# The RMSNorm gain as a per-partition scale where transposed activations leave PSUM, and the first loads in a new order on two queues

## The chip, the cores and the metric

One core of one Trainium2 chip runs the whole kernel. The metric is the device time of one execution in microseconds (us).

## What is computed

A decoder trunk of two layers on x with 256 rows (tokens) and 1024 columns, float32. What this change touches is the norm at the head of each layer and the products that read it:

```
for l in range(DEPTH):                       # 2
    h = rms_norm(x, norm_g[l])               # x * rsqrt(mean(x*x) + eps) * g
    proj = h @ w_in[l]                       # split into q, kv, gates, ... for four token mixers
    outs = (nsa(...), conv(...), stick_breaking(...), s5(...))   # each times silu of a gate
    mixed = sum over m of sigmoid(merge[m]) * (outs[m] @ w_branch[l, m])
    x = x + mixed @ w_out[l]
```

## The kernel before

The engines have short names in the profile: PE is TensorE, ACT is ScalarE, DVE is VectorE, POOL is GpSimd, and SP issues most loads. The 256 tokens are two tiles of 128 partitions, called t=0 and t=1. Weights come in 78 tiles a layer of 512 KB (`raw`, three buffers). Each is split into two parts: a rounded copy `hi` (ACT, L148) and the remainder `lo` = raw - hi (L150), on DVE or, for tiles 2, 4, 79, 81 and 95, on POOL. A product of activations and weights is three matmuls, hi by hi, lo by hi and hi by lo. A load for a buffer waits until the remainder three tiles earlier is done.

The head of a layer goes through these steps for each of its two token tiles:

- `norm_square` adds up the squares of a row (ACT, L533), with halves of 512 columns in layer 0 and quarters of 256 in layer 1, as the output projection of the layer before delivers them. DVE adds the parts (L538), POOL raises the sum to the power -1/2 (L539).
- `norm_scale` (L547) makes h = x * rs * g on DVE, in two halves of 512 columns. The gain g lies in `ng`, a 128x1024 tile that a load has broadcast over all partitions.
- `norm_transpose` turns the eight 128x128 pieces of h on PE (L555) into two PSUM banks `hT`, four pieces in each. Per bank, ACT rounds 128x512 into `hh` (L558), and DVE puts the remainder of the same bank into `hl` (L559). `hh` and `hl` are what every projection reads.

The projection reads q first, then ksw (keys), then vsw (values) and so on. Query and key outputs are then normed, rotated and transposed: ACT squares (L565), DVE sums (L567), POOL takes the power (`rsq`, `rsk`, L569), DVE multiplies (L576 to L587), PE transposes into `qTp` and `kTp` (L592), and the first scores are `sc` (L703).

The order of SP and POOL is the program's own. The order of PE, DVE and ACT is set by a scheduler of the framework, which runs a model of the timeline when the kernel is built. Each engine executes its list in order. At the start the loads are issued by SP one after another: x in two halves, constants, positions, gain and weights in turns. PE meanwhile runs 13 matmuls on zeros.

Of the kernel before, what the change touches and what calls it, by code (L numbers as in the profile page):

```python
# [31 lines left out]
# columns of the input projection  # L32
# [3 lines left out]
# parameters packed per partition  # L36
# [9 lines left out]
_CS = [("ident", 128), ("invf", 32), ("tau", 32)]  # L46
# [15 lines left out]
def slot_plan():  # L62
    """The weight tiles in the order of their use: (key, kind, columns)."""
# [51 lines left out]
class Weights:  # L115
    """Streams the weight tiles and splits each into two float32r parts."""
# [40 lines left out]
    def advance(self, g):  # L157
        """Emits the splits of the tiles after tile g, as far as the tiles in use leave room."""
        end = min(g + self.depth - 1, min(self.parts_in_use, default=g) + self.depth, DEPTH * NSLOT)
        while self.ns < end:  # L160
            self.prefetch(self.ns + 1)
            self._split()
        self.prefetch(min(max(self.ns, g + 1) + self.ahead, DEPTH * NSLOT))
# [14 lines left out]
def tile_hybrid_trunk(ctx: ExitStack, tc: tile.TileContext, x, pos, cst, msk, wq, ws, ng, pk, w1, gw, out):  # L178
# [25 lines left out]
    def stack(name, parts):  # L204
        """For each of the four groups of 32 rows, those rows of the three parts one below the other."""
        out = []
        for pair in range(2):
            t = fp.tile([96, 2, 512], F32R, name=f"{name}{pair}", tag="f")
            for j in range(2):
                q = 2 * pair + j  # L210
                for i, part in enumerate(parts):
                    nc.sync.dma_start(t[32 * i:32 * i + 32, j, :].bitcast(F32),
                                      part[32 * q:32 * q + 32].bitcast(F32))
            out.append(t)
        return out
# [54 lines left out]
    # tiles with blocks that stay zero  # L270
# [7 lines left out]
    # rotary tables: [token, (tile 0, tile 1, compressed), 2, 32]  # L278
# [43 lines left out]
    def load_ng(l, L):  # L322
        L["ng"] = fp.tile([P, D], F32, name=f"ng{l}", tag="f")
        nc.sync.dma_start(L["ng"], ng[l:l + 1, :].to_broadcast([P, D]))
# [31 lines left out]
    def prep_s5(l, L):  # L356
        """Phases of the state rotation; the decay and the output matrices."""
# [39 lines left out]
    def prep_s5_tables(l, L):  # L397
        """Rotation by 16 i + j steps, from those by 16 i and by j."""
# [126 lines left out]
    def norm_square(l, t, u, n):  # L525
        """Adds up the squares of the u-th of n parts of a row."""
# [5 lines left out]
        with tc.high_priority():  # L532
            A.activation(h[:, cols], xs[:, t, cols], AF.Square, scale=1.0 / 32, accum_out=ss[:, u:u + 1])  # L533
# [8 lines left out]
    def norm_scale(l, t):  # L542
        h, rs = Ls[l]["norm"][t]
        for c in range(2):
            cols = slice(c * 512, c * 512 + 512)
            with tc.high_priority():
                V.scalar_tensor_tensor(h[:, cols], xs[:, t, cols], rs, Ls[l]["ng"][:, cols], op0=ALU.mult, op1=ALU.mult)  # L547

    def norm_transpose(l, t, act):
        hh, hl = act  # L550
        h = Ls[l]["norm"][t][0]
        for c in range(2):
# [3 lines left out]
            dst = (slice(None), slice(4 * c, 4 * c + 4), slice(t * P, (t + 1) * P))  # L556
            with tc.high_priority():
                A.copy(hh[dst], ps)  # L558
                V.tensor_sub(hl[dst], ps, hh[dst].bitcast(F32))  # L559

# [1 line left out]
    def nsa_rope(l, t, name, ps, L, kinds, scale, dst):  # L562
        """QK norm, rotation and transposition of four heads; kinds: the gain rows of the heads."""
# [127 lines left out]
    def nsa_full(l, L, acc, t, bs):  # L691
        """Causal attention of the branches bs (0 selected, 1 window) for query tile t."""
# [290 lines left out]
    def prepare(l):  # L983
        """What a layer needs apart from its activations."""
# [9 lines left out]
    ng0 = fp.tile([P, D], F32, name="ng0", tag="f")  # L994
    Ls[0]["ng"] = ng0
    halves = [slice(c * 512, c * 512 + 512) for c in range(2)]
    for c in halves:
        nc.sync.dma_start(xs[:, 0, c], x[0:P, c])
    nc.sync.dma_start(cs, cst)
    nc.sync.dma_start(posi, pos)  # L1000
    nc.sync.dma_start(ng0[:, halves[0]], ng[0:1, halves[0]].to_broadcast([P, 512]))
    W.prefetch(1)
    nc.sync.dma_start(ng0[:, halves[1]], ng[0:1, halves[1]].to_broadcast([P, 512]))
# [33 lines left out]
    for l in range(DEPTH):  # L1037
# [82 lines left out]
        if more:  # L1120
            load_ng(l + 1, Ls[l + 1])
# [24 lines left out]
def _constants():  # L1146
# [3 lines left out]
    def put(n, v):  # L1150
        o, w = CS[n]
        c[:v.shape[0], o:o + w] = v

    put("ident", np.eye(P))
    inv = np.power(10000.0, -np.arange(32) / 32).astype(np.float32)
# [12 lines left out]
def _layout(x, positions, norm_g, w_in, nsa_qk_g, nsa_cmp_pe, nsa_cmp_w1, nsa_cmp_w2, sc_conv_w, s5_a_re, s5_a_im,  # L1168
            s5_log_dt, s5_b_re, s5_b_im, s5_c_re, s5_c_im, s5_d, s5_glu_w, s5_glu_b, w_branch, w_out):
    Ld = DEPTH  # L1170
    cst, msk = _constants()
# [52 lines left out]
    arrays = dict(x=x[0], pos=pos, cst=cst, msk=msk, wq=wq, ws=ws, ng=norm_g, pk=pk, w1=w1, gw=gw)  # L1224
# [22 lines left out]
```

## Time and profile before

| What | us |
| --- | --- |
| Runs | 583.56, 584.46, 586.82 |
| Median of the runs | 584.46 |
| Profiled execution, first to last instruction | 583.8 |
| PE busy | 553.6 (95%) |
| DVE busy | 435.6 (75%) |
| POOL busy | 283.0 (48%) |
| ACT busy | 266.4 (46%) |

The profiled execution's own device time is not listed apart from its span. The mean granted clock of PE over the span is 0.976. Timelines give the start of an instruction, counted from the first one, its duration, what it is, and in brackets how long its engine had been idle before it and what ended that. Matmuls are pipelined, so the step from one start to the next is the pace, not the duration. [...]

### The profile page before, as it was taken

The numbers are of one execution on the slowest core, as the hardware profiler recorded it, in microseconds if no ns is written. First come the engines' busy times: TensorE is split into PE (matmuls) and PEld (weight loads), VectorE is DVE, ScalarE is ACT, GpSimd is POOL, SyncE is SP. The second block draws the span as 40 slices with busy tenths as digits, with TensorE's granted clock in tenths as the row PEclk, the third lists the DMA queues.
The fourth block names the chain that finished last, engine by engine and source line by source line (L and its number), as shares of the span: only waits on it lengthen the run. The fifth ranks groups of instructions, "written<-read, shape, count | busy, mean of one in ns | idle before, by whom it ended". The sixth has DMA issues, their size and how long they took to land.

```text
span 583.8 us, 11199 instructions
## 1 busy us (share of the span) xinstructions
PE 553.6 (95%) x4417; PEld 515.9 (88%) x4417; DVE 435.6 (75%) x649; ACT 266.4 (46%) x438; POOL 283.0 (48%) x314
## 2 busy tenths in 40 slices
PE   6897999999799999969798999999999999999997
PEld 3897988889598899969698999889889899999997
DVE  3997776898898676786469974859999685677782
ACT  4658453544243446424254474633534354444440
POOL 3699835546554476899934420214356500132230
PEclk8997999999899999979899999999999999999999
DMA  8664153534345364545444653454334456555531
GB/s 266 224 227 142 38 199 116 192 113 170 115 144 183 108 232 146 187 159 175 153 149 133 233 177 96 145 164 154 131 125 138 170 169 197 186 183 177 207 129 56
DMA packets 28709, 93.54 MB, mean 160 GB/s; under 512 B 3824, under 2 KB 5104, under 8 KB 28656
## 3 DMA queue, kind: packets, MB, share of 16 engines
q1 hardware_dynamic: 28656, 92.82, 47.1%
q8 instruction: 35, 0.57, 0.4%
q14 instruction: 18, 0.15, 0.1%
HBM read 88.61 MB, written 1.05 MB: 154 GB/s over the span
## 4 chain that ended last, share of the span: by engine, by line
PE 65%; POOL 19%; DVE 7%; issue 6%; DMA 2%; ACT 1%; SPq 0%; DVEq 0%; POOLq 0%; ACTq 0%
PE mg L492 19%; PE wo L482 6%; PE br L937 5%; PE z L492 4%; POOL cy L289 3%; PE sbk L492 2%; PE s5u L492 2%; PE sbv L482 2%; PE xin L492 2%; PE cg L492 2%; PE bg L492 2%; PE sc L703 2%; POOL mt L286 2%; PE nsacc L740 2%; POOL cy L286 2%
## 5 line engine op out<-in xcount | busy, mean ns | idle before, releaser
L150 DVE TENSOR_TENSOR lo<-raw,hi 128x1024 fp32r<-128x1024 f32 (+1 forms) x151 | 202.3, 1345 | 44.3 <-ACT hi L148 44.1
L148 ACT CAST hi<-raw 128x1024 fp32r<-128x1024 f32 (+1 forms) x154 | 161.0, 1049 | 153.8 <-PE mg L492 56.9
L492 PE MATMUL mg<-hh,hi 128*128 128x256 f32 x512 | 146.0, 285 | 5.6 <-DVE mt L940 5.6
L492 PE MATMUL mg<-hh,lo 128*128 128x256 f32 x512 | 145.2, 284 | 0.0
L492 PE MATMUL mg<-hl,hi 128*128 128x256 f32 x512 | 145.1, 283 | 0.0
L492 PEld LDWEIGHTS mg<-hh,hi 128*128 128x128 f32 x512 | 97.9, 191 | 11.0 <-DVE mt L940 5.8
L492 PEld LDWEIGHTS mg<-hh,lo 128*128 128x128 f32 x512 | 97.5, 190 | 0.4 <-issue 0.4
L492 PEld LDWEIGHTS mg<-hl,hi 128*128 128x128 f32 x512 | 97.4, 190 | 0.4 <-issue 0.4
L286 POOL TENSOR_TENSOR mt<-mt,mt 128x512 f32<-128x512 f32 x14 | 22.9, 1633 | 78.8 <-DVE mt L940 78.8
L482 PE MATMUL wo<-hi,mx 128*128 128x256 f32 x256 | 48.1, 288 | 4.1 <-ACT mx L956 4.1
L289 POOL TENSOR_TENSOR cy<-cy 128x256 f32<-128x256 f32 x16 | 23.0, 1437 | 52.9 <-DVE cy L865 49.1
L482 PEld LDWEIGHTS wo<-hi,mx 128*128 128x128 f32 x256 | 40.8, 194 | 4.7 <-ACT mx L956 4.5
L937 PE MATMUL br<-oh,hi 128*128 128x256 f32 x128 | 36.0, 281 | 0.5 <-ACT g L922 0.5
L492 PE MATMUL z<-hl,hi 128*128 128x256 f32 x128 | 36.2, 283 | 0.0
L492 PE MATMUL z<-hh,lo 128*128 128x256 f32 x128 | 36.1, 282 | 0.0
L492 PE MATMUL z<-hh,hi 128*128 128x256 f32 x128 | 36.0, 281 | 0.0
L937 PE MATMUL br<-oh,lo 128*128 128x256 f32 x128 | 36.0, 281 | 0.0
L937 PE MATMUL br<-ol,hi 128*128 128x256 f32 x128 | 35.9, 281 | 0.0
L482 PE MATMUL wo<-lo,mx 128*128 128x256 f32 x128 | 35.9, 286 | 0.0
L286 POOL TENSOR_TENSOR s5a<-s5a,s5b 128x256 f32<-128x256 f32 x16 | 19.6, 1222 | 26.3 <-DMA raw<-in_ws_dram 13.9
L859 DVE TENSOR_TENSOR_SCAN s5b<-r,s5a 128x256 f32<-128x256 f32 x32 | 20.3, 677 | 14.2 <-POOL s5a L289 14.2
L492 PEld LDWEIGHTS z<-hl,hi 128*128 128x128 f32 x128 | 24.1, 188 | 0.8 <-issue 0.8
(334 smaller groups left out, 1430.2 us busy)
## 6 DMA issues: line engine op xcount, KB each, us to landing
raw<-in_ws_dram SPq DMA_DIRECT2D x152, 512.0 KB, 3.9
raw<-in_wq_dram SPq DMA_DIRECT2D x4, 536.0 KB, 4.9
w<-in_w_dram SPq DMA_DIRECT2D x4, 512.0 KB, 6.1
b<-bh SPq DMA_DIRECT2D x16, 64.0 KB, 2.0
u<-uh SPq DMA_DIRECT2D x16, 64.0 KB, 2.0
gw<-in_gw_dram SPq DMA_DIRECT2D x2, 512.0 KB, 5.5
out_dram<-xs SPq DMA_DIRECT2D x8, 128.0 KB, 1.7
pk<-in_pk_dram SPq DMA_DIRECT2D x2, 322.0 KB, 3.5
```

The lines of the kernel that those rows point to most:

```text
L148: self.nc.scalar.copy(hi[:, :w], t[:, :w])
L150: sub.tensor_sub(lo[:, :w], t[:, :w], hi[:, :w].bitcast(F32))
L286: G.tensor_add(o, a, b)
L289: G.tensor_sub(o, a, b)
L482: T.matmul(ps[:, :width], lhsT=act(4 * h + kk)[ia][:, tt], rhs=w[iw][:, kk, :], start=n == 0, stop=n == last)
L492: T.matmul(ps, lhsT=w[:, k, :], rhs=a[:, k, :], start=n == 0, stop=n == last)
L703: T.matmul(sc[kh].rearrange("p (b g k) -> p b g k", b=nb, g=2)[:, :, g, :], lhsT=qT[iq][rows[kh], g, t * P:(t + 1) * P], rhs=kT[ik][rows[k ...
L740: T.matmul(acc[rows[kh], :, t * P:(t + 1) * P], lhsT=v[:, c, b * P + 64 * kh:b * P + 64 * kh + 64], rhs=ps4[kh][:, c, 2 * i:2 * i + 2, :], ...
L859: V.tensor_tensor_scan(y[:, ri, :], L["r"][:, pr:pr + 1].to_broadcast([P, S]), a[:, ri, :], 0.0, op0=ALU.mult, op1=ALU.add)
L937: T.matmul(ps[:, j, :], lhsT=w[:, 2 * m + k, :], rhs=a[:, k, :], start=n == 0, stop=n == 5)
```

## The change

- The gain is 16 more columns in the table of constants `cs` (192 to 208 columns): column 8l+k holds for each partition the gain of piece k of layer l. The tile `ng` and its loads go, 512 KB a layer.
- h becomes x * rs alone, a TENSOR_SCALAR.
- `norm_transpose` applies the gain where a piece leaves PSUM: per piece one ACT copy of 128x128 with the gain as scale and one DVE instruction hT * g - hh. There are 32 and 32 of them where there were 8 and 8.
- In layer 0 the square of the second half goes from ACT to DVE.
- Loads at the start: the second half of x on ACT's queue, and the first two weight tiles earlier on SP's.

```diff
-_CS = [("ident", 128), ("invf", 32), ("tau", 32)]
+_CS = [("ident", 128), ("gain", 16), ("invf", 32), ("tau", 32)]
...
-    def load_ng(l, L):
-        L["ng"] = fp.tile([P, D], F32, name=f"ng{l}", tag="f")
-        nc.sync.dma_start(L["ng"], ng[l:l + 1, :].to_broadcast([P, D]))
...
         with tc.high_priority():
-            A.activation(h[:, cols], xs[:, t, cols], AF.Square, scale=1.0 / 32, accum_out=ss[:, u:u + 1])
+            if l == 0 and u == 1:
+                V.scalar_tensor_tensor(h[:, cols], xs[:, t, cols], 1.0 / D, xs[:, t, cols], op0=ALU.mult, op1=ALU.mult,
+                                       accum_out=ss[:, u:u + 1])
+            else:
+                A.activation(h[:, cols], xs[:, t, cols], AF.Square, scale=1.0 / 32, accum_out=ss[:, u:u + 1])
...
             with tc.high_priority():
-                V.scalar_tensor_tensor(h[:, cols], xs[:, t, cols], rs, Ls[l]["ng"][:, cols], op0=ALU.mult, op1=ALU.mult)
+                V.tensor_scalar(h[:, cols], xs[:, t, cols], rs, None, op0=ALU.mult)
...
-            dst = (slice(None), slice(4 * c, 4 * c + 4), slice(t * P, (t + 1) * P))
             with tc.high_priority():
-                A.copy(hh[dst], ps)
-                V.tensor_sub(hl[dst], ps, hh[dst].bitcast(F32))
+                for k in range(4):
+                    g = C("gain")[:, 8 * l + 4 * c + k:8 * l + 4 * c + k + 1]
+                    hi, lo = (v[:, 4 * c + k, t * P:(t + 1) * P] for v in (hh, hl))
+                    A.activation(hi, ps[:, k, :], AF.Copy, scale=g)
+                    V.scalar_tensor_tensor(lo, ps[:, k, :], g, hi.bitcast(F32), op0=ALU.mult, op1=ALU.subtract)
...
-    ng0 = fp.tile([P, D], F32, name="ng0", tag="f")
-    Ls[0]["ng"] = ng0
-    halves = [slice(c * 512, c * 512 + 512) for c in range(2)]
-    for c in halves:
-        nc.sync.dma_start(xs[:, 0, c], x[0:P, c])
+    nc.sync.dma_start(xs[:, 0, :512], x[0:P, :512])
+    nc.scalar.dma_start(xs[:, 0, 512:], x[0:P, 512:])
     nc.sync.dma_start(cs, cst)
+    W.prefetch(1)
     nc.sync.dma_start(posi, pos)
-    nc.sync.dma_start(ng0[:, halves[0]], ng[0:1, halves[0]].to_broadcast([P, 512]))
-    W.prefetch(1)
-    nc.sync.dma_start(ng0[:, halves[1]], ng[0:1, halves[1]].to_broadcast([P, 512]))
     W.prefetch(2)
...
-        if more:
-            load_ng(l + 1, Ls[l + 1])
+    put("gain", norm_g.reshape(DEPTH, KC, P).transpose(2, 0, 1).reshape(P, -1))
```

The scheduler orders PE, DVE and ACT anew around the head of each layer; POOL's list keeps its order. In the new list of PE, 139 matmuls stand ahead of the first transposition of a key tile (kTp00) and 269 ahead of the second (kTp01), the 13 on zeros counted; before, they were 192 and 249. Ahead of the first scores stand 277 (before 279). Two places follow.

DVE in layer 0, from the remainders of t=0 on (the first two digits behind a name are layer and token tile, hT000 and hT001 are the two banks of t=0; lo0, lo1, lo3 are remainders of weight tiles). Before:

```order
L559 TENSOR_TENSOR hl0_153<-hT000_162,hh0_152 128x4x128 [waits Activation_49]
L559 TENSOR_TENSOR hl0_153<-hT001_169,hh0_152 128x4x128 [waits Activation_49]
L312 TENSOR_SCALAR ang_184<-ang_184 128x96 [waits Pool_49]
L150 TENSOR_TENSOR lo1_198<-raw1_127,hi1_197 128x1072 [waits DMAHW7_49,Activation_49]
L538 SCALAR_TENSOR_TENSOR ss01_204<-ss01_204 128x1 [waits Activation_49]
L319 TENSOR_SCALAR ropeS_112<-ropeS_112 128x3x32 [waits Activation_49]
L547 SCALAR_TENSOR_TENSOR h01_203<-xs_93,ss01_204,ng0_118 128x512 [waits DMAHW0_49,Pool_49]
L547 SCALAR_TENSOR_TENSOR h01_203<-xs_93,ss01_204,ng0_118 128x512
```

and now, from the third piece (of pieces 0 to 3 of a bank) of t=0 on:

```order
L538 SCALAR_TENSOR_TENSOR ss01_213<-ss01_213 128x1 [waits DVE_49,Activation_49]
L561 SCALAR_TENSOR_TENSOR hl0_150<-hT000_159,cs_94,hh0_149 128x128 [waits Activation_49]
L547 TENSOR_SCALAR h01_212<-xs_93,ss01_213 128x512 [waits Pool_49]
L547 TENSOR_SCALAR h01_212<-xs_93,ss01_213 128x512
L561 SCALAR_TENSOR_TENSOR hl0_150<-hT001_172,cs_94,hh0_149 128x128 [waits Activation_49]
L319 TENSOR_SCALAR ropeS_112<-ropeS_112 128x3x32 [waits Activation_49]
L561 SCALAR_TENSOR_TENSOR hl0_150<-hT000_159,cs_94,hh0_149 128x128 [waits Activation_49]
L341 TENSOR_TENSOR gS0_236<-qk0_129,ropeS_112 128x192 [waits DMAHW0_49,DVE_49]
L341 TENSOR_TENSOR gS0_236<-qk0_129,ropeS_112 128x192
L342 TENSOR_TENSOR gS0_236<-qk0_129,ropeS_112 128x64
L150 TENSOR_TENSOR lo3_254<-raw3_189,hi3_253 128x1024 [waits DMAHW1_49,Activation_49]
L561 SCALAR_TENSOR_TENSOR hl0_150<-hT001_172,cs_94,hh0_149 128x128 [waits Activation_49]
```

Both remainders of t=0 stood ahead of h of t=1 (h01); now three of the eight stand behind it.

DVE at the boundary of the layers (hT100 and hT101 are the two banks of t=0 in layer 1, h11 is h of t=1, lo82 a weight remainder). Before:

```order
L965 SCALAR_TENSOR_TENSOR xs_93<-wo031_3708,xs_93 128x256 [waits PE_49]
L559 TENSOR_TENSOR hl1_3667<-hT100_3721,hh1_3666 128x4x128 [waits Activation_49]
L559 TENSOR_TENSOR hl1_3667<-hT101_3728,hh1_3666 128x4x128 [waits Activation_49]
L538 SCALAR_TENSOR_TENSOR ss11_3527<-ss11_3527 128x1 [waits Activation_49]
L547 SCALAR_TENSOR_TENSOR h11_3526<-xs_93,ss11_3527,ng1_3454 128x512 [waits Pool_49]
L547 SCALAR_TENSOR_TENSOR h11_3526<-xs_93,ss11_3527,ng1_3454 128x512 [waits DVE_49]
L150 TENSOR_TENSOR lo82_3770<-raw82_3704,hi82_3769 128x1024 [waits DMAHW2_49,Activation_49]
```

and now, from the small sum for t=1 on, which follows the second piece of both banks:

```order
L538 SCALAR_TENSOR_TENSOR ss11_3546<-ss11_3546 128x1 [waits Activation_49]
L561 SCALAR_TENSOR_TENSOR hl1_3686<-hT100_3740,cs_94,hh1_3685 128x128 [waits Activation_49]
L561 SCALAR_TENSOR_TENSOR hl1_3686<-hT101_3753,cs_94,hh1_3685 128x128 [waits Activation_49]
L547 TENSOR_SCALAR h11_3545<-xs_93,ss11_3546 128x512 [waits Pool_49]
L547 TENSOR_SCALAR h11_3545<-xs_93,ss11_3546 128x512 [waits DVE_49]
L150 TENSOR_TENSOR lo82_3801<-raw82_3723,hi82_3800 128x1024 [waits DMAHW7_49,Activation_49]
L561 SCALAR_TENSOR_TENSOR hl1_3686<-hT100_3740,cs_94,hh1_3685 128x128 [waits Activation_49]
L561 SCALAR_TENSOR_TENSOR hl1_3686<-hT101_3753,cs_94,hh1_3685 128x128 [waits Activation_49]
```

The last piece of each bank of t=0 now follows h11 and lo82.

## Rows read from the trace of the kernel before

**Rows 1.** The page: the span.

```profile
span 583.8 us, 11199 instructions
```

**Rows 2.** Stretches: us, busy time and count of each engine, clock, share of DMA, GB/s.

```profile
51.00:54.00 3.00, 3.00 (x15) 2.50 (x15) 2.93 (x8) 1.87 (x3) 2.92 (x4) 0.50 0.51 171
...
156.70:160.10 3.40, 3.40 (x11) 1.55 (x12) 3.37 (x5) 0.62 (x1) 2.03 (x3) 0.50 0.44 154
303.00:308.00 5.00, 5.00 (x44) 5.00 (x44) 2.65 (x4) 2.65 (x4) 2.08 (x2) 1.00 0.33 111
```

**Rows 3.** Timeline of PE, start to 51 us: start, duration, instruction, count, idle before it.

```profile
11.95 1.24 PE L482 MATMUL q<-hi,hh 128*128 128x268 f32 x4
...
44.88 0.41 PE L592 MATMUL kTp<-cs,m1k 128*128 128x128 f32 x2 [1.14 <-DVE m1k L587]
...
45.25 0.28 PE L492 MATMUL sbq<-hh,lo 128*128 128x256 f32 x1
...
48.19 0.28 PE L492 MATMUL sbk<-hh,hi 128*128 128x256 f32 x1
...
50.82 0.58 PE L703 MATMUL sc<-kT,qT 64*128 64x256 f32 x1 [2.23 <-DVE qTl L595]
```

**Rows 4.** Timeline of ACT, first 10 us.

```profile
4.47 0.63 ACT L533 ACTIVATE h<-xs 128x512 f32<-128x512 f32 x1 [0.36 <-DMA xs<-in_x_dram]
...
9.24 1.08 ACT L148 CAST hi<-raw 128x1072 fp32r<-128x1072 f32 x1 [4.05 <-DMA raw<-in_wq_dram]
```

**Rows 5.** Timeline of DVE, first 25 us.

```profile
8.08 0.75 DVE L547 SCALAR_TENSOR_TENSOR h<-xs,ss,ng 128x512 f32<-128x512 f32 x1 [2.70 <-DMA ng<-in_ng_dram]
...
12.23 1.41 DVE L559 TENSOR_TENSOR hl<-hT,hh 128x512 fp32r<-128x512 f32 x2
...
16.01 3.52 DVE L547 SCALAR_TENSOR_TENSOR h<-xs,ss,ng 128x512 f32<-128x512 f32 x2 [0.44 <-POOL ss L539]
...
22.79 1.66 DVE L318 COPY ropeC<-ropeC 128x96 f32<-128x96 f32 x1
```

**Rows 6.** Groups of lines of ACT, then DVE: busy us, mean ns of one, idle before.

```profile
L715 ACT ACTIVATE e<-sc,m 128x128 f32<-128x128 f32 x16 | 5.7, 373 | 1.3 <-DVE m L711 1.3
...
L558 ACT CAST hh<-hT 128x512 fp32r<-128x512 f32 x8 | 4.6, 584 | 3.6 <-PE hT L555 3.5
...
L559 DVE TENSOR_TENSOR hl<-hT,hh 128x512 fp32r<-128x512 f32 x8 | 5.3, 682 | 0.5 <-ACT hh L558 0.5
...
L582 DVE TENSOR_TENSOR sqq<-q,gS 128x128 f32<-128x128 f32 x8 | 1.9, 279 | 0.0
...
L906 DVE TENSOR_SCALAR s5th<-s5th 128x512 f32<-128x512 f32 x2 | 0.9, 428 | 2.8 <-ACT s5th L904 2.8
```

**Rows 7.** Timeline of POOL, 16 to 32 us.

```profile
16.32 2.66 POOL L150 TENSOR_TENSOR lo<-raw,hi 128x1024 fp32r<-128x1024 f32 x1 [0.35 <-ACT hi L148]
21.95 2.42 POOL L150 TENSOR_TENSOR lo<-raw,hi 128x1024 fp32r<-128x1024 f32 x1 [2.97 <-ACT hi L148]
...
31.46 2.04 POOL L569 TENSOR_TENSOR rsk<-ssk,mhalf 128x4 f32<-128x4 f32 x1
```

**Rows 8.** Timeline of DVE at the layer boundary.

```profile
305.94 3.68 DVE L547 SCALAR_TENSOR_TENSOR h<-xs,ss,ng 128x512 f32<-128x512 f32 x2 [0.68 <-POOL ss L539]
...
313.98 3.55 DVE L547 SCALAR_TENSOR_TENSOR h<-xs,ss,ng 128x512 f32<-128x512 f32 x2 [0.67 <-POOL ss L539]
317.45 1.22 DVE L150 TENSOR_TENSOR lo<-raw,hi 128x1024 fp32r<-128x1024 f32 x1
```

**Rows 9.** Timeline of POOL at the layer boundary.

```profile
306.49 2.59 POOL L150 TENSOR_TENSOR lo<-raw,hi 128x1072 fp32r<-128x1072 f32 x1 [0.58 <-ACT hi L148]
313.39 0.56 POOL L539 TENSOR_TENSOR ss<-ss,mhalf 128x1 f32<-128x1 f32 x1 [4.31 <-DVE ss L538]
313.91 2.41 POOL L150 TENSOR_TENSOR lo<-raw,hi 128x1024 fp32r<-128x1024 f32 x1
```

**Rows 10.** Timeline of PE at the layer boundary.

```profile
311.97 0.76 PE L482 MATMUL q<-hi,hh 128*128 128x268 f32 x4 [1.57 <-ACT hh L558]
```

More of the change, by code (lines that the diff above doesn't have):

```diff
@@ L177, in tile_hybrid_trunk @@
 @with_exitstack
-def tile_hybrid_trunk(ctx: ExitStack, tc: tile.TileContext, x, pos, cst, msk, wq, ws, ng, pk, w1, gw, out):
+def tile_hybrid_trunk(ctx: ExitStack, tc: tile.TileContext, x, pos, cst, msk, wq, ws, pk, w1, gw, out):
     nc = tc.nc
@@ L1143, in tile_hybrid_trunk, with _constants @@
             W.advance((l + 1) * NSLOT - 1)
-def _constants():
+def _constants(norm_g):
     t = np.arange(P)
@@ L1170, in _layout @@
     Ld = DEPTH
-    cst, msk = _constants()
+    cst, msk = _constants(norm_g)
     p = positions[0]
@@ L1223, in _layout @@
     gw = s5_glu_w.reshape(Ld, 2, P, 512).transpose(0, 2, 1, 3)
-    arrays = dict(x=x[0], pos=pos, cst=cst, msk=msk, wq=wq, ws=ws, ng=norm_g, pk=pk, w1=w1, gw=gw)
+    arrays = dict(x=x[0], pos=pos, cst=cst, msk=msk, wq=wq, ws=ws, pk=pk, w1=w1, gw=gw)
     return {k: np.ascontiguousarray(v) for k, v in arrays.items()}
```

## The prediction

> **What bounds the kernel now.** I read the page first: TensorE (PE) is busy for nearly the whole span of 583.8 us [rows 1], so a change counts only where PE stands still or runs at its lower clock. [...] The timeline of PE shows what came before: the first q matmul at 11.95, then, after a dense run, idle 1.14 us ahead of 44.88 and 2.23 us ahead of 50.82 [rows 3]. At 50.82 the clock falls. It did not fall after the 1.57 us of idle at 311.97, where layer 1 starts [rows 10]. So about 12 us at the start, the gaps at 44 to 51 with what the clock takes behind them, and 1.57 us at the boundary are what the edited lines could move. Everything else is PE at its pace.
>
> The timelines of the feeding engines tell why. At the start h waits for the broadcast gain (idle 2.70 before 8.08), and ScalarE (ACT) waits 4.05 us for the first weight tile [rows 4, 5]. Second, h of t=1 takes 3.52 us for two instructions at 16.01, and 3.68 and 3.55 at the boundary [rows 5, 8], though the first one at 8.08 took 0.75. Beside each long pair lies a POOL remainder of a weight tile (16.32, 306.49, 313.91) [rows 7, 9]: VectorE (DVE) stands until POOL is done. The small COPY at 22.79 does the same: 1.66 us, ending with POOL's 21.95+2.42 [rows 5, 7].
>
> **The change part by part.** The profiled execution's span is 583.8; its own device time is not listed, and the median of the runs, 584.46, lies 0.7 above it. I work in differences and add them to 584.46. All results inside 0.5% (2.92 us) are "same": a measurement of this kernel can hardly tell them from none.
>
> *Gain loads gone, first loads reordered.* Both halves of x are there at about 4.0 (the second was used at 4.47 [rows 4]). Squares run side by side on ACT and DVE to about 4.9; with the power on POOL (0.56 [rows 9]) h can start at 5.8. As TENSOR_SCALAR a half takes 0.43 (the L906 row [rows 6]), so h is done at 6.6 where it was 11.1. The transposes follow the warm-up, the first weight tile, which came 1.16 us behind the gain's first half (9.24 against 8.08 [rows 4, 5]), now follows the constants, by my estimate at 6 to 6.5, and q starts near 8.3 instead of 11.95: 3.6 us ahead. The gain load that goes at the boundary I cost at nothing: h waits there 0.68 for POOL, not for it [rows 8].
>
> *The copies out of PSUM.* Before, a bank took one ACT copy and one DVE subtraction of 512 columns. Now each takes four and four of 128, and in the order every further ACT copy of a bank waits for DVE's last one on it. No row has these forms. The ACT copy: below, a quarter of the whole-bank copy (0.584, L558), 0.15; above, 0.37, that of 128 columns with a per-partition operand (L715). I take 0.37, the nearest form. DVE: 0.28 (128x128, L582) to 0.68 (the whole bank, L559); I take 0.34, near the first [rows 6]. A step of one bank is then 0.37+0.34 and two hand-overs, about 0.8 (DVE waits 0.67 for a power that takes 0.56, so two cost 0.1 [rows 8, 9]); four steps of two interleaved banks are 3.2 to 3.6 us a tile. Before, hi-copy and subtraction of a tile overlapped in about 1.9. Alone that is 1.5 us for each of four tiles, and a gain of zero is the other end if other work fills the steps. What decides is what DVE has *between* these steps, since it runs in order.
>
> *Start, the sum.* DVE's order from q's start: remainder of tile 0 to 8.4 (its cast is done by 7.1, the remainder takes 1.2 to 1.3), piece 0 of both banks to 9.1, remainder 1 behind its cast to 10.7, the square of t=1 (0.75 taken for it, as for h) to 11.5, piece 1 to 12.2, the small sum, piece 2 of the first bank to 12.9. The power that follows the sum costs 0.67 [rows 8], so h of t=1 can start at 13.2 (16.01 before). POOL has its tile 2 ready at that time and takes it first, for 2.4 us. DVE stands, h of t=1 ends at 16.5 (19.53 before). Behind it in the order stand the last remainders of t=0: with the rope products and weight tile 3 ahead of the final one, that is ready at about 20.4, where all of t=0's were at 13.64 [rows 5]. Then gC and eight remainders of t=1 with the q and k work between: the last at about 33. POOL's power for k, behind its chain of phases, starts at 32.3 (31.46 before) and takes 2.04 [rows 7], so k's rotated tile, a product of some 0.4 later, is there at about 34.8. In the order that transposition of k (kTp00) has 139 matmuls ahead of it. Before, the 249 that stand ahead of kTp01 were done at 43.74, the start of the idle time at 44.88; at 0.118 each (25 steps from 45.25 to 48.19 [rows 3]) PE had done 173 at 34.8. The new kernel is 34 matmuls, 4.0 us, behind.
>
> But it then has no gap to fall into: from 34.8 the 138 matmuls to the first score take 16.3, to 51.1, about when its inputs come (50.82 before). In the kernel before the clock is low from there for nearly 7 us, and PE does 5 matmuls a us instead of 8.8, a loss of 3.0 [rows 2]. Kept high, PE ends 2.7 ahead. Against that I set one stretch of 3.4 us at the low clock (as at 156.7 [rows 2]), worth 1.7, for the stalls before 35. **Start: -1.0**, bounds -4 (h of t=1 not held up) and +3 (two long low stretches, 2x3.0 against the 2.7).
>
> *Boundary.* h of t=0 now needs 2x0.43 from 305.94, done before POOL's tile 79 can hold it: 2.8 us gained on DVE. It lets the square of t=1, the cast of tile 81 and so the first copy move to 309.6, and q starts at 310.4, as soon as PE has ended wo: the 1.57 us go. Then the steps bite. Pieces 0 to 2 of both banks end at 312.9 with DVE's xs, its remainders and the square in between. The order then has h of t=1 (two), weight remainder 82, and only behind these the remainders of piece 3. At about 312.6 POOL's power for t=1 ends and POOL goes straight into its tile 81, whose cast I put at 309.5, as it did before at 313.91, 0.07 us ahead of h's start at 313.98 [rows 8, 9]. h is held to 315.1 and done at 315.9, tile 82 takes 1.22 [rows 8] to 317.1, piece 3's first remainder is there at 317.5. PE meanwhile can issue 22 matmuls from 310.4 and idles twice for about 2.3 us. Before, from 311.97 to 317.45 it issued some 44. That is 22x0.118 = 2.6 us lost, the 1.57 included. With 2.6 us of work in 7 the clock should fall, as it did behind 2.23 us of idle at 50.82; one stretch of 3.4 us costs 1.7. **Boundary: +4.3**, bounds +0.5 (h not held) and +6 (a long low stretch, 3.0, and more stalls in t=1's copies).
>
> [...]
>
> [...]
>
> *Rest of layer 1.* Reordered, no new wait seen: 0, bounds +-1.
>
> **Sum:** 584.46 - 1.0 + 4.3 + 0 = 587.8.
>
> **Rivals.**
> (A) h gets ahead of POOL at the boundary, or the clock stays up there. For it: 0.07 us decided at 313.91. Against it: DVE now arrives later than the power's end, not earlier. Boundary +0.6 or +2.6; with start -1.0 or -2.7 the time is 584.1 or 584.4. The same.
> (B) Faster: the three early microseconds are kept. For it: q starts 3.6 us earlier, and 6.4 us of idle and low clock lie ahead at 44 to 58. It needs tile 2's cast to end after the power of t=1, so that h is done at 14.1 and t=0's last remainder near 18. Start -4, boundary +0.6: 581.0. Its point of decision is whether POOL's tile 2 starts behind h.
> (C) Slower still: the copies starve PE at both places long enough for long low-clock stretches. Start +2, boundary +6: 592.5.
> (D) The change does not do what it says: not open, since the order shows 32 and 32 short copies, no gain load, and TENSOR_SCALAR.
>
> **How the numbers follow.** Forecast 0.40 (0.07 of it within 0.5%), A 0.29, B 0.20, C 0.11. Faster 0.20, same 0.29+0.07 = 0.36, slower 0.33+0.11 = 0.44. The range 580.5 to 592.5 reaches from B to C; the forecast's own is 585.5 to 591.
>
> **What would show it.** Right: q begins near 8.3, the last t=0 remainder comes at 19 to 21, little PE idle at 44 to 51, clock 1.00 from 51 to 57, and around 315 PE waiting for hl over 2 us behind an h of more than 2 us. Wrong: h of t=1 under 0.5 us in either layer, a clock of 1.00 behind the boundary, or copies much off 0.37 and 0.34.

## The result, and the profile after

The changed kernel took 590.58 us, the median of 8 runs (586.05 to 592.28); the kernel before, in 8 runs beside them, 584.59 (583.56 to 586.82). The ratio, taken over all runs, is 1.0084, with a 95% interval of 1.0057 to 1.0110: slower by 0.84% (the two medians alone lie 6.0 us, 1.0%, apart). The median is inside the forecast's own range of 585.5 to 591. The profiled execution took 591.84 with a span of 590.1, 6.3 more than the span of before [rows 1].

The page: the span, and busy time of each engine (share of the span, count).

```profile
span 590.1 us, 11232 instructions
PE 559.4 (95%) x4417; PEld 519.3 (88%) x4417; DVE 435.6 (74%) x677; ACT 270.9 (46%) x458; POOL 284.9 (48%) x314
```

The new forms, in the groups of lines of ACT and DVE (busy us, mean ns of one, idle before and what ended it):

```profile
L560 ACT ACTIVATE hh<-hT,cs 128x128 fp32r<-128x128 f32 x32 | 10.9, 366 | 17.4 <-DVE hl L561 9.6 <-PE hT L555 7.4
...
L561 DVE SCALAR_TENSOR_TENSOR hl<-hT,cs,hh 128x128 fp32r<-128x128 f32 x32 | 10.5, 343 | 4.6 <-ACT hh L560 4.4
L547 DVE TENSOR_SCALAR h<-xs,ss 128x512 f32<-128x512 f32 x8 | 7.7, 1007 | 1.8 <-POOL ss L539 1.8
```

The pieces cost 0.37 and 0.34, as taken [rows 6]. ACT's copies stood idle 17.4 us, 9.6 of it behind DVE: the hand-overs. And h has a mean of 1007 ns where 428 was the free price [rows 6], since two of the four pairs (the two halves of h) were held by POOL (2.99 and 2.97 us; the other two took 0.88).

**The start.** DVE's timeline:

```profile
6.13 0.88 DVE L547 TENSOR_SCALAR h<-xs,ss 128x512 f32<-128x512 f32 x2 [0.75 <-POOL ss L539]
...
14.31 2.99 DVE L547 TENSOR_SCALAR h<-xs,ss 128x512 f32<-128x512 f32 x2 [0.42 <-POOL ss L539]
...
19.67 0.34 DVE L561 SCALAR_TENSOR_TENSOR hl<-hT,cs,hh 128x128 fp32r<-128x128 f32 x1
...
35.15 2.90 DVE L150 TENSOR_TENSOR lo<-raw,hi 128x1024 fp32r<-128x1024 f32 x2
...
39.37 0.15 DVE L570 TENSOR_SCALAR ssq<-ssq 128x4 f32<-128x4 f32 x1
```

POOL's, from 14 us:

```profile
14.23 2.39 POOL L150 TENSOR_TENSOR lo<-raw,hi 128x1024 fp32r<-128x1024 f32 x1
...
39.60 1.01 POOL L571 TENSOR_TENSOR rsq<-ssq,mhalf 128x4 f32<-128x4 f32 x1 [2.64 <-DVE ssq L570]
...
61.37 1.51 POOL L286 TENSOR_TENSOR BB<-bm,bm 64x128 f32<-64x128 f32 x2
```

PE's, from 8 to 63 us:

```profile
8.40 0.39 PE L478 MATMUL q<-hi,hh 128*128 128x268 f32 x1 [0.63 <-ACT hh L560]
10.10 0.39 PE L478 MATMUL q<-hi,hh 128*128 128x268 f32 x1 [1.31 <-ACT hh L560]
...
18.00 0.59 PE L478 MATMUL q<-hi,hl 128*128 128x268 f32 x1 [1.50 <-DVE hl L561]
...
33.60 0.44 PE L594 MATMUL kTp<-cs,m1k 128*128 128x128 f32 x2 [0.78 <-DVE m1k L589]
...
50.26 0.38 PE L705 MATMUL sc<-kT,qT 64*128 64x256 f32 x1
...
62.93 0.53 PE L462 MATMUL bbp<-cs,BB 128*128 128x128 f32 x2 [1.74 <-POOL BB L286]
```

q starts 3.55 us earlier than before [rows 3] and stands after each piece; h of t=1 is held from 14.31 to POOL's end (14.23+2.39) and its second half runs free (0.48); the last remainder of t=0 ends at 20.0; kTp00 comes at 33.60; the first score at 50.26 waits for nothing (2.23 before [rows 3]). That far it is the predicted path. Then the last row: PE stands 1.74 us at 62.93 for BB, a matrix that POOL builds for the s5 mixer. The table of stretches (length, busy time and count of PE, weight loads, DVE, ACT, POOL, granted clock as a share of the full one, share of DMA, GB/s) shows what follows it:

```profile
10.00:20.00 10.00, 5.72 (x20) 4.60 (x21) 8.64 (x19) 6.00 (x14) 6.91 (x8) 0.60 0.61 195
20.00:35.00 15.00, 14.22 (x111) 14.02 (x111) 13.11 (x41) 7.16 (x17) 11.17 (x16) 0.93 0.59 198
35.00:50.00 15.00, 15.00 (x127) 14.87 (x127) 14.04 (x28) 11.55 (x19) 11.94 (x12) 1.00 0.69 220
50.00:58.00 8.00, 7.28 (x54) 6.40 (x53) 7.60 (x19) 6.99 (x17) 7.56 (x13) 1.00 0.34 116
58.00:63.00 5.00, 3.26 (x71) 2.81 (x70) 4.75 (x10) 1.52 (x9) 4.65 (x7) 1.00 0.01 3
63.00:66.50 3.50, 3.50 (x18) 3.50 (x19) 1.71 (x4) 2.13 (x4) 3.34 (x6) 0.52 0.16 37
```

The clock is 1.00 from 50 to 58, where it was 0.50 before [rows 2], but 0.52 from 63 to 66.5, where it was 1.00. That last stretch in the kernel before:

```profile
63.00:66.50 3.50, 3.50 (x32) 3.50 (x31) 2.37 (x6) 1.68 (x3) 3.34 (x6) 1.00 0.00 0
```

**The boundary.** DVE's timeline:

```profile
307.83 0.88 DVE L547 TENSOR_SCALAR h<-xs,ss 128x512 f32<-128x512 f32 x2 [0.68 <-POOL ss L539]
...
309.71 2.48 DVE L150 TENSOR_TENSOR lo<-raw,hi 128x1024 fp32r<-128x1024 f32 x1 [0.66 <-ACT hi L148]
...
314.50 2.97 DVE L547 TENSOR_SCALAR h<-xs,ss 128x512 f32<-128x512 f32 x2
317.40 1.21 DVE L150 TENSOR_TENSOR lo<-raw,hi 128x1024 fp32r<-128x1024 f32 x1
318.53 0.60 DVE L561 SCALAR_TENSOR_TENSOR hl<-hT,cs,hh 128x128 fp32r<-128x128 f32 x2
```

POOL's and, below it, ACT's:

```profile
313.91 0.56 POOL L539 TENSOR_TENSOR ss<-ss,mhalf 128x1 f32<-128x1 f32 x1 [2.81 <-DVE ss L538]
314.44 2.36 POOL L150 TENSOR_TENSOR lo<-raw,hi 128x1024 fp32r<-128x1024 f32 x1
```

```profile
314.70 1.04 ACT L148 CAST hi<-raw 128x1024 fp32r<-128x1024 f32 x1 [0.54 <-DMA raw<-in_ws_dram]
315.65 0.62 ACT L560 ACTIVATE hh<-hT,cs 128x128 fp32r<-128x128 f32 x2
```

PE's, and its stretch at the low clock:

```profile
312.09 0.29 PE L478 MATMUL q<-hi,hh 128*128 128x268 f32 x1
...
316.07 0.59 PE L478 MATMUL q<-hi,hh 128*128 128x268 f32 x1 [1.35 <-ACT hh L560]
...
318.93 0.59 PE L478 MATMUL q<-hi,hl 128*128 128x268 f32 x1 [0.28 <-DVE hl L561]
```

```profile
315.70:322.50 6.80, 6.16 (x27) 5.86 (x27) 3.43 (x5) 0.57 (x3) 1.09 (x1) 0.50 0.43 136
```

h of t=0 is free, q starts without its 1.57 us [rows 10], POOL's tile 81 starts 0.06 us ahead of h of t=1 and holds it to 316.8 (314.44+2.36), so that h ends at 317.5, and the fourth pieces come behind h and tile 82 [compare rows 8, 9]. The hold that h of t=0 had before has moved: the remainder of tile 80 on DVE now starts at 309.71, while POOL is at its tile 79 (308.39 to 311.09), and takes 2.48 us, where that of tile 82 takes 1.21.

To place the loss I count the matmuls that PE has started up to some times, from the same view with stretches that begin at 0; a minus means behind the kernel before. At full clock one is 0.118 us [rows 3]; between 55 and 70 us many are shorter (62 of the changed kernel's, from 58.58 on, take 2.24 us together), so there the first matmul on BB (bbp) serves as the mark, though its place in PE's list moves by up to 12 matmuls between these kernels. g12 is counted without the 4 matmul instructions that spread its gain.

| Kernel (profiled execution) | at 35 | first bbp | at 100 | at 310 | at 550 | started from 310 to 330 |
| --- | --- | --- | --- | --- | --- | --- |
| before, number started | 179 | 62.98 us | 674 | 2221 | 4159 | 146 |
| changed | -28 | 60.75 | -16 | -16 | -52 | 119 |
| e1_whole | +1 | 58.70 | 0 | +4 | +23 | 161 |
| e2_no81 | -32 | 61.16 | -6 | -2 | -40 | 130 |
| e4_l1old | -28 | 61.29 | +5 | +2 | +13 | 153 |
| e6_l0old | +1 | 59.42 | +9 | +6 | -14 | 132 |
| e7_no24 | -8 | 59.04 | +14 | -14 | -48 | 114 |
| e8_81first | -30 | 60.98 | -16 | -12 | -30 | 134 |
| g12_gain_in_psum | +16 | 56.41 | +31 | +23 | +48 | 169 |

The changed kernel is 2.2 us ahead at bbp. The wait of 1.74 us takes most of that, and in the low stretch behind it PE starts 18 matmuls where before it started 32 from 63 to 66.5: 1.7 us. It is 16 behind (1.9 us) at 100 and at 310, loses 27 (3.2 us) in the 20 us of the boundary and 9 more (1.1 us) after it: 6.1 of the 6.3.

### The profile page after: what moved, and what is told of

Read it like the earlier page. It is cut to its first block, busy times and chain, and to the rows that moved or that the text cites. A ratio compares the mean times of both kernels' runs of the same rounds, so it can differ in the third digit from the quotient of the medians.

```text
span 590.1 us, 11232 instructions
## 1 busy us (share of the span) xinstructions
PE 559.4 (95%) x4417; PEld 519.3 (88%) x4417; DVE 435.6 (74%) x677; ACT 270.9 (46%) x458; POOL 284.9 (48%) x314
## 4 chain that ended last, share of the span: by engine, by line
PE 64%; POOL 19%; DVE 9%; issue 4%; DMA 2%; ACT 1%; DVEq 0%; POOLq 0%; ACTq 0%
PE mg L488 20%; PE wo L478 6%; PE z L488 5%; PE br L939 4%; DVE lo L150 3%; POOL mt L286 3%; PE s5u L488 2%; PE sbv L478 2%; PE xin L488 2%; PE bg L488 2%; PE cg L488 2%; POOL cy L289 2%; POOL rot L292 2%; PE nsacc L742 2%; PE sc L705 2%
## 5 line engine op out<-in xcount | busy, mean ns | idle before, releaser
L488 PEld LDWEIGHTS z<-hh,hi 128*128 128x128 f32 x128 | 24.2, 189 | 1.2 <-issue 1.2
```

Source lines behind the costliest of these rows:

```text
L488: T.matmul(ps, lhsT=w[:, k, :], rhs=a[:, k, :], start=n == 0, stop=n == last)
```

## The experiments

Each ratio is against runs of the kernel before on the same chip. Where an experiment keeps the old lines for some token tiles, it also loads the gain for those.

**e1_whole: the change with whole-bank copies.**

```diff
-                for k in range(4):
-                    g = C("gain")[:, 8 * l + 4 * c + k:8 * l + 4 * c + k + 1]
-                    hi, lo = (v[:, 4 * c + k, t * P:(t + 1) * P] for v in (hh, hl))
-                    A.activation(hi, ps[:, k, :], AF.Copy, scale=g)
-                    V.scalar_tensor_tensor(lo, ps[:, k, :], g, hi.bitcast(F32), op0=ALU.mult, op1=ALU.subtract)
+                A.copy(hh[dst], ps)
+                V.tensor_sub(hl[dst], ps, hh[dst].bitcast(F32))
```

(`dst` is the same slice as in the kernel before.)

> The changed kernel with the whole-bank copies of before (one ACT copy and one DVE subtraction of 512 columns a bank); the gain is left out, so its output lacks it. Loads, the short h and the square on DVE stay. Theory H (the short copies of t=0 end up behind h of t=1, which POOL holds, and the clock falls behind the wait): both places recover, h of t=1 is still held about 2.4 us but nothing of t=0 stands behind it; 579 to 583, so 2 to 6 us under the kernel before. Rival L (the loads, the second queue or the extra DVE square cost the time): stays near 590. A gain of zero against the kernel before (584 to 585) would say that the early start is absorbed later.

Measured: 583.52, ratio 0.9982 (0.9959 to 1.0005), a little above the 579 to 583 of its theory. All else that the change does gains at most 0.4%; the pieces, with the order that the scheduler makes around them, cost 0.84 + 0.18 = 1.0%, 6 us. The two were not run apart: kTp00 stands behind 186 matmuls here and behind 139 in the changed kernel. DVE's timeline at the boundary shows where the pieces cost it:

```profile
309.85 0.68 DVE L559 TENSOR_TENSOR hl<-hT,hh 128x512 fp32r<-128x512 f32 x1
...
310.77 0.68 DVE L559 TENSOR_TENSOR hl<-hT,hh 128x512 fp32r<-128x512 f32 x1
...
312.26 3.03 DVE L547 TENSOR_SCALAR h<-xs,ss 128x512 f32<-128x512 f32 x2 [0.67 <-POOL ss L539]
```

h of t=1 is held as long as in the changed kernel, yet PE starts 161 matmuls from 310 to 330 instead of 119: both remainders are out before h. The tile 80 remainder takes 2.48 us here too. So these holds by themselves are not the loss (PE waits 0.64 us for h here, at 315.04, and 0.31 before); they harm most what the pieces leave behind them.

**e4_l1old and e6_l0old: the change in one layer alone.** e4 keeps the old gain and copies in layer 1, e6 all of the old head of layer 0, its loads and both squares on ACT included.

```diff
+OLD = [(1, 0), (1, 1)]
...
+                if (l, t) in OLD:
+                    V.scalar_tensor_tensor(h[:, cols], xs[:, t, cols], rs, Ls[l]["ng"][:, cols], op0=ALU.mult, op1=ALU.mult)
...
+            if (l, t) in OLD:
+                dst = (slice(None), slice(4 * c, 4 * c + 4), slice(t * P, (t + 1) * P))
+                with tc.high_priority():
+                    A.copy(hh[dst], ps)
+                    V.tensor_sub(hl[dst], ps, hh[dst].bitcast(F32))
+                continue
```

For e6 the first line is `OLD = [(0, 0), (0, 1)]`, and the loads of the start stand as before.

> The changed kernel in layer 0; in layer 1 the gain is loaded, multiplied into h and copied by whole banks as before. It takes the boundary's part out. Theory H: the boundary is worth 4.4 us of the 6, so 585.5 to 587, with 1 to 2 us lost at the start, and the clock at 1.00 behind the boundary. Rival C (the short copies cost alike in both layers, 3 us each): 587.5.

> Layer 0 as before (its loads, gain loaded at the start, whole-bank copies, both squares on ACT), layer 1 as changed. It leaves the boundary alone. Theory H: all of the boundary's 3.3 to 4.7 us and none of the start's: 587.5 to 589.5. If start and boundary only add up, this and the run with layer 1 as before together exceed the kernel before by as much as the changed kernel does (about 5 to 6 us).

Measured: e4 585.86, 1.0021 (0.9999 to 1.0043); e6 588.70, 1.0056 (1.0032 to 1.0080). The parts add up, 0.21 + 0.56 = 0.77 against 0.84%. Layer 1 is the larger one, 3.3 us. Layer 0 is no gain, and e4's profiled execution, one of its faster (584.21), tells how near it was. POOL's and PE's timelines there:

```profile
39.59 1.01 POOL L585 TENSOR_TENSOR rsq<-ssq,mhalf 128x4 f32<-128x4 f32 x1 [2.64 <-DVE ssq L584]
...
59.19 1.32 POOL L287 TENSOR_TENSOR BB<-bm,bm 64x128 f32<-64x128 f32 x2
```

```profile
61.29 0.66 PE L467 MATMUL bbp<-cs,BB 128*128 128x128 f32 x4
```

With the same lists on all four engines up to 70 us, BB is done at 60.5 instead of 62.9, PE does not wait for it, and no low clock follows (31 matmuls from 63 to 66.5 at 1.00, instead of 18 at 0.52). It is 5 matmuls ahead at 100, the changed kernel 16 behind: 2.5 us on one wait and the clock behind it. The late second power for q is not what differs: it starts at 39.59 here, at 39.60 in the changed kernel. From 47.1 on, where the second power for k ends in both, POOL takes 13.4 us to the end of BB here and 15.8 in the changed kernel, with single instructions (bm) at 0.40 in the one and 1.38 in the other; what stretched them stays open. e2_no81 (below), which has these lists too, shows wait and clock apart:

```profile
63.37 0.44 PE L462 MATMUL bbp<-cs,BB 128*128 128x128 f32 x2 [1.76 <-POOL BB L286]
```

PE waits as long as in the changed kernel, the clock stays at 1.00 behind it, and at 100 it is 6 matmuls behind. By these single profiles the wait is about half of the 2.5 us and the clock the other half.

e6 tells how much one profile can say. The table of stretches gives for it:

```profile
50.00:58.00 8.00, 7.42 (x77) 6.85 (x77) 7.37 (x16) 5.58 (x18) 7.58 (x12) 1.00 0.33 119
...
310.00:330.00 20.00, 17.10 (x133) 16.28 (x134) 15.08 (x39) 10.02 (x27) 4.93 (x4) 1.00 0.46 158
```

Up to 70 us its lists are those of the kernel before, but for the order of three score matmuls. Yet the clock stays at 1.00 where the kernel before had it at 0.50 [rows 2], and PE reaches bbp 3.6 us sooner. Around the boundary its lists are those of the changed kernel, h of t=1 is held as long (2.98 us at 311.87) and PE waits 1.28 us for hh and 1.45 for hl, yet the clock stays at 1.00 there too. So neither low stretch belongs to every execution of its list. Without the low clock the boundary costs 14 matmuls (146 - 132), 1.7 us, about half of what it costs the changed kernel.

**e3_loads: the kernel before with the first loads in the new order alone** (x in two halves on two queues, positions behind the first weight tile).

```diff
-    for c in halves:
-        nc.sync.dma_start(xs[:, 0, c], x[0:P, c])
+    nc.sync.dma_start(xs[:, 0, halves[0]], x[0:P, halves[0]])
+    nc.scalar.dma_start(xs[:, 0, halves[1]], x[0:P, halves[1]])
     nc.sync.dma_start(cs, cst)
-    nc.sync.dma_start(posi, pos)
     nc.sync.dma_start(ng0[:, halves[0]], ng[0:1, halves[0]].to_broadcast([P, 512]))
     W.prefetch(1)
+    nc.sync.dma_start(posi, pos)
```

> The kernel before with only the first loads changed: the second half of x on ACT's queue, the gain's first half ahead of the first weight tile, positions later. Gain loads, long h and whole-bank copies stay. Theory H: the gain still lands near 7.5 and h waits for it, so 583.5 to 585.5, no change. Rival L (second queue and order of loads matter by themselves): more than 2 us either way.

Measured: 586.00, 1.0021 (1.0001 to 1.0042), half a microsecond above what was expected. The order of the loads brings nothing while the gain's loads stand in it.

**e8_81first and b8_81first: POOL's tile 81 ahead of the power for t=1,** in the changed kernel (e8) and in the kernel before (b8). A call behind the last matmuls of the layer's output projection releases the weight tile there.

```diff
+        if then:
+            then()
...
-        out_part(l, 3, s3, mx, 1, lambda: norm_transpose(l + 1, 0, act) if more else None)
-        done_n(l, ("wo", 3))
-        if more:
-            W.advance((l + 1) * NSLOT - 1)
+        def next_tile():
+            done_n(l, ("wo", 3))
+            if more:
+                W.advance((l + 1) * NSLOT)
+
+        out_part(l, 3, s3, mx, 1, lambda: norm_transpose(l + 1, 0, act) if more else None, next_tile)
```

> The changed kernel with one thing moved: at the boundary POOL has weight tile 81's remainder in its list ahead of the power for t=1 instead of behind it. DVE's and ACT's lists around it stay. Theory H: POOL's remainder then runs from about 311.2 to 313.6, while DVE has only copies out of PSUM and is held for nothing but xs; h of t=1 takes 0.9 us instead of 3.0, the last remainders of t=0 are out 2 us earlier, PE's delay at the boundary goes from 3.3 to about 1.5; 587 to 589. Rival C (the short copies are the cost by themselves): 590 to 591.

> The kernel before, with only POOL's weight tile 81 ahead of the power for t=1 at the boundary. h of t=1 there then takes 1.5 us instead of 3.6. PE waited only 0.31 us for it, so 0 to 0.5 us faster: 583.8 to 584.5, no difference that a measurement shows. More than 2 us faster would say that the hold already cost the kernel before more than its waits show.

Measured: e8 587.47, 1.0047 (1.0026 to 1.0067); b8 584.27, 0.9977 (0.9957 to 0.9997). DVE's and POOL's timelines of e8:

```profile
314.62 0.88 DVE L547 TENSOR_SCALAR h<-xs,ss 128x512 f32<-128x512 f32 x2 [0.15 <-POOL ss L539]
...
316.55 0.60 DVE L561 SCALAR_TENSOR_TENSOR hl<-hT,cs,hh 128x128 fp32r<-128x128 f32 x2
```

```profile
307.91 6.02 POOL L150 TENSOR_TENSOR lo<-raw,hi 128x1072 fp32r<-128x1072 f32 x2 [0.61 <-ACT hi L148]
```

h takes 0.88, the fourth pieces come 2.0 us earlier (0.5 of it because e8 is that much ahead at h of t=0), the low clock lasts 3.4 us (316.4 to 319.8) instead of 6.8, and PE starts 134 matmuls instead of 119: 1.8 us. In the runs it is 0.84 - 0.47 = 0.37% (2.2 us), though the two intervals overlap. That is the most that the hold of h costs, clock included: e6 has the hold and, at a clock of 1.00, starts 132. The same edit is worth 0.23% in the kernel before, so what it brings more under the change, 0.14%, is not clear of noise. What is left between 134 and the 161 of e1, 3.2 us, is the chain of pieces with h free, and the 3.4 us at the low clock that came with it.

**e2_no81: tile 81's remainder on DVE.**

```diff
-    W = Weights(nc, tc, raw, hip, lop, wq, ws, 3, 5, (2, 4, 79, 81, 95), (17, 87))
+    W = Weights(nc, tc, raw, hip, lop, wq, ws, 3, 5, (2, 4, 79, 95), (17, 87))
```

> The changed kernel with the remainder of weight tile 81 on DVE (1.2 us there) instead of POOL. Theory H: h of t=1 at the boundary takes 0.9 us instead of 3.0, the last remainders of t=0 come about 1 us earlier net, PE idles less before them and the clock may stay at 1.00 behind 315; the boundary's 4.4 us shrink to 0.5 to 3, the time is 586 to 589. Rival C (the alternation of short copies is itself the cost, whoever holds h): 590 to 592, as DVE has 1.2 us more.

Measured: 590.59, 1.0092 (1.0060 to 1.0125), a miss: as slow as the change. h is free (0.88), but the remainder now stands in DVE's list ahead of the first pieces. DVE's and PE's timelines:

```profile
310.65 1.21 DVE L150 TENSOR_TENSOR lo<-raw,hi 128x1024 fp32r<-128x1024 f32 x1
```

```profile
312.17 0.39 PE L478 MATMUL ksw<-hi,hl 128*128 128x256 f32 x1 [1.07 <-DVE hl L561]
```

PE starts 130 matmuls at the boundary, 11 more than the change, and loses 22 more from 330 to 550 (from -18 to -40). One later wait, 1.4 us for a weight remainder on DVE at 477, is part of it; the rest stays open.

**e7_no24, e10_no24_81first, e11_l1old_no24_81first: tiles 2 and 4 on DVE too,** alone, with e8's edit, and with layer 1 as before besides.

```diff
-    W = Weights(nc, tc, raw, hip, lop, wq, ws, 3, 5, (2, 4, 79, 81, 95), (17, 87))
+    W = Weights(nc, tc, raw, hip, lop, wq, ws, 3, 5, (79, 81, 95), (17, 87))
```

> The changed kernel with the remainders of weight tiles 2 and 4 on DVE, so that POOL holds nothing at the start; the boundary stays as changed. DVE gets 2.4 us more work there. Theory H: h of t=1 takes 0.9 us instead of 3.0 and the 2.1 us COPY 0.4, the last remainder of t=0 comes 1 us or so earlier, PE is behind by 2 to 3 us instead of 3.6 at 35; 588 to 590, 1 to 2 us under the changed kernel. If it is no faster, the start's loss is in the pieces and the order, not in the hold.

> The changed kernel with both holds away: tiles 2 and 4 on DVE, tile 81 ahead of the power for t=1. Theory H: the gain of the run with 81 first (587.5) and that of tiles 2 and 4 add up, 585.5 to 587.5. What then remains over 584.5 is the price of the short copies themselves.

> Layer 0 as changed, layer 1 as before (gain loaded, whole-bank copies), tiles 2 and 4 on DVE, tile 81 ahead of the power: all that the runs before point to as cheap. Theory H: the layer-1 form without its price and the start without its hold, 582.5 to 584.5; the run with only layer 1 as before gave 585.9. If over 585, the early start is worth nothing with short copies.

Measured: e7 589.03, 1.0079 (1.0056 to 1.0102); e10 586.27, 1.0025 (1.0003 to 1.0047); e11 584.37, 0.9997 (0.9980 to 1.0015). Without the two holds e7 is 14 ahead at 100 where the change is 16 behind, but 14 behind again at 310 (its clock is 0.51 from 193.9 to 197.3; why stays open). All three keep short pieces, and none is faster than the kernel before.

**e5_t0new: only t=0 of layer 0 in the new form.** The list is `OLD = [(0, 1), (1, 0), (1, 1)]`, and the gain is loaded behind the third weight tile.

> Only the first tile of layer 0 as changed (early loads, short h, gain where it leaves PSUM); its gain row is loaded behind the third weight tile for t=1, which is done as before, and so is layer 1. Theory H (what hurts at the start is that DVE has the short remainders of t=1 between the rope work, so POOL's second power for q comes late): that power near 37 again, PE ahead of before by 2 to 4 us at 60; 580.5 to 583.5. Rival (t=0's own short copies behind h of t=1 are the start's cost): 585 to 586, like the run with layer 1 alone as before.

Measured: 591.76, 1.0104 (1.0070 to 1.0138), a miss for its theory and for the rival. The second power for q came at 38.70, not near 37, though t=1 has no pieces; but a new wait came first, so the run does not settle whether the pieces of t=1 do harm. DVE's, ACT's and PE's timelines:

```profile
15.02 3.48 DVE L553 SCALAR_TENSOR_TENSOR h<-xs,ss,ng 128x512 f32<-128x512 f32 x2 [0.29 <-POOL ss L544]
```

```profile
18.80 0.37 ACT L574 ACTIVATE hh<-hT,cs 128x128 fp32r<-128x128 f32 x1 [3.80 <-DVE hl L575]
```

```profile
19.22 0.59 PE L483 MATMUL q<-hi,hh 128*128 128x268 f32 x1 [3.90 <-ACT hh L574]
```

The longer, held h of t=1 stands ahead of pieces of t=0, and PE stops for 3.90 us at once. Here it is what is queued *ahead of* a piece that counts.

**g12_gain_in_psum: the same aim by another way.** The kernel before keeps its whole-bank copies. Layer 0's gain comes as one row of 4 KB, two matmuls with a row of ones spread it over the partitions into two PSUM banks, and h reads it there. With it: x on two queues, and b8's edit.

```diff
+    nc.sync.dma_start(grow, ng[0:1, :])
...
+    for c in halves:
+        ps = pj.tile([P, 512], F32, tag="pj", name="ngp")
+        T.matmul(ps, lhsT=ones, rhs=grow[:, c], start=True, stop=True)
+        Ls[0]["ngp"].append(ps)
...
+                V.scalar_tensor_tensor(h[:, cols], xs[:, t, cols], rs, Ls[0]["ngp"][c] if l == 0 else Ls[l]["ng"][:, cols],
+                                       op0=ALU.mult, op1=ALU.mult)
```

> A version drawn from the runs: the copies stay whole-bank and h keeps its gain, but in layer 0 the gain row comes as one 4 KB load and two one-row matmuls spread it over the partitions in PSUM, where h reads it; x comes on two queues; POOL's tile 81 goes ahead of the power for t=1; layer 1 otherwise as before. Theory H: h of t=0 near 6, as early as changed, h of t=1 not held (one operand from SBUF, one from PSUM) or held once, nothing of t=0 behind it, and q00 done 3 us earlier than before; 580.5 to 583.5. If it only equals the kernel before (584 to 585), the early microseconds are absorbed by the work that comes later, as the run with whole-bank copies and no gain (583.5) hinted.

Measured: 579.98, 0.9912 (0.9891 to 0.9934), faster than both kernels and than its own 580.5 to 583.5. DVE's and POOL's timelines, and a stretch:

```profile
14.50 1.40 DVE L547 SCALAR_TENSOR_TENSOR h<-xs,ss,ngp 128x512 f32<-128x512 f32 x2
15.81 0.91 DVE L319 TENSOR_SCALAR ropeS<-ropeS 128x96 f32<-128x96 f32 x1
```

```profile
14.22 2.42 POOL L150 TENSOR_TENSOR lo<-raw,hi 128x1024 fp32r<-128x1024 f32 x1
```

```profile
50.00:58.00 8.00, 7.89 (x110) 7.54 (x110) 6.97 (x14) 4.95 (x18) 7.57 (x12) 1.00 0.07 26
```

h of t=0 is no earlier than before (8.09 against 8.08, not "near 6"): PE spreads the gain only from 6.77 on, behind its matmuls on zeros. But h of t=1 runs through in 1.40 us beside POOL's tile 2. PE reaches bbp 6.6 us sooner than before, is 31 matmuls (3.7 us) ahead at 100, and there is no low clock at 50 to 58 (as in e6, whose list is the old one). Which of the three edits brings how much of the 0.88% was not run apart, beyond b8's 0.23%.

## Why the prediction was right, and what was off

*Direction and class: right.* Slower by more than 0.5%, and by its main mechanism, pieces of t=0 behind a held h at the boundary. That the time itself fell into the range is in part the range's width: the profile puts the three terms at +1.9, +3.2 and +1.1 where the sum had -1.0, +4.3 and 0.

*The boundary, +4.3: right in size.* It measured +3.2 in the profile; by the runs e4 puts layer 1's whole share at 0.84 - 0.21 = 0.63%, 3.7 us, and e6 at 0.56%, 3.3. The race of rival A came out as argued: POOL first, by 0.06 us. That is not luck: POOL's power releases both, and POOL is first by 0.06 to 0.08 us in e1 and e7 too (312.20 against 312.26, 314.15 against 314.23). Some details failed. Of the 2.8 us that h of t=0 was to give DVE, 1.3 went to the remainder of tile 80, held in its place. The point "PE waiting for hl over 2 us" did not show: PE waited 1.35 us for the fourth copy of hh, since ACT's list has the cast of tile 82, late by its load, ahead of it; the low clock then stretched PE's work until only 0.28 was left of the wait for hl. And that stretch was 6.8 us, not 3.4, the value that stood in the upper bound, and in e6 there was none. That the hold itself is only part (at most 1.8 of the 5 us between 119 and 161) the prediction did not separate; its own list of steps had both. The 44 matmuls that it gave the kernel before from 311.97 to 317.45 are 41 in the trace. And a held h did gain a little: the pairs took 2.99 and 2.97 us instead of 3.52 and 3.55.

*The start, -1.0: the step that failed.* The path to 58 us held: q at 8.4 (8.3 said), h of t=1 from 14.31 to 17.3 (13.2 to 16.5), the last remainder of t=0 at 20.0 (20.4), kTp00 at 33.6 (34.8), 28 matmuls behind at 35 (34 said), clock 1.00 from 51 to 57, 2.2 us ahead at bbp (2.7). Wrong was "Kept high, PE ends 2.7 ahead. Against that I set one stretch of 3.4 us": the sum stopped at the first score. POOL was not followed beyond rsk00. Its second power for q (`rsq` of t=1) stood 2.64 us for DVE, which at 35 to 39 us has two weight remainders and more ahead of the sum. It came at 39.60 (36.97 before), and BB, at the end of POOL's list of phases, at 62.9 (59.7 before). PE waited 1.74 and got a stretch at the low clock. The term measured +1.9 instead of -1.0; in e4's profile, where the power was as late but BB came 2.4 us sooner, it was -0.6, and by e4's runs 0.21%, +1.2. So the late power brings BB near PE's need, and how long POOL's instructions behind it take decides. Such a race fits the spread of the changed kernel's runs (two of eight at 586.05 and 586.75 with a mean clock of 0.979, the others from 590.07, five of them at 0.970), though only one of them has a profile. The gain in the term, the clock "kept high" from 51, is uncertain as well: e6 has that clock with the old layer 0, reaches bbp 3.6 us sooner than the profile of before, and is 9 matmuls (1.1 us) ahead at 100. So much of any single profile is scatter.

*The rest, 0: about +1.1,* just past its bounds.

*The shorter h, and rival B.* Eight halves of h at 0.43 us instead of 0.75 [rows 5, 6] are 2.6 us; by this estimate all of them on the path would have given 581.9. e1, which has that gain and the early loads and no pieces, took 583.52: of the 2.6 us about 1 was found, and its interval includes none. The early start was taken up later: e1 reaches bbp some 4 us sooner (58.70) and is level at 100, with waits for DVE of 0.85 us at 62.44 and 0.80 at 65.43. Rival B fell at its point of decision: POOL's tile 2 started at 14.23, 0.08 us ahead of h.

## What to carry to other kernels

The copy that was cut into pieces which alternate between two engines was as slow as everything that DVE, working in order, had queued between the pieces (they cost 0.37 and 0.34 us each, but the last remainder of t=0 ended at 20.0 us instead of 13.64 [rows 5]): read the list, not the durations. The operand saved on h, which POOL held up, saved little where h started second (3.55 us became 2.97); POOL's remainder ahead of the power (0.88 in e8), or another place for the operand (1.40 in g12), did more. And follow a shifted start to the last consumer on every engine, not to the first point where PE has caught up. A low stretch of the clock seen in one profile is not yet a cost of that kernel: another execution of the same list may lack it (behind waits of 1.74 and 1.76 us at bbp it was 0.52 in the changed kernel and 1.00 in e2).

## What the runs showed of the hardware that I had not expected

An instruction of DVE with one operand in PSUM was not held by POOL's remainder: in g12 two halves of h took 1.40 us inside POOL's 14.22 to 16.64, while the form with both operands in SBUF took 3.52 beside the same tile [rows 5] and the very next DVE instruction, from SBUF alone, ended only with POOL at 16.7. One operand in PSUM was here a way around the hold, 1.40 us instead of 3.52.

Behind bbp and at the boundary the low clock came in stretches of 3.4 us (63.1 to 66.5 in the changed kernel, 316.4 to 319.8 in e8) and of 6.8 (315.7 to 322.5 in the changed kernel), each time behind a few microseconds in which PE had stood still for part of the time: in the changed kernel it was busy 3.26 of 5.00 us from 58 to 63 and 3.55 of 4.70 from 311 to 315.7, in e8 1.80 of 3.00 from 313 to 316. The wait of 1.74 us cost about as much again in clock (18 matmuls instead of 32, 1.7 us). It did not always go so: behind the 1.76 us in e2 (at 63.37) and the 1.28 and 1.45 at e6's boundary the clock stayed at 1.00.
